# A float32 transformer trunk on one core: the high parts of the mixers' and cross attention's weights written by GpSimd in place of ScalarE

## The chip, the cores and the metric

The kernel runs on one core of a Trainium2 chip. A core has five engines that work at the same time, each through its own queue of instructions in order: TensorE (PE, with PEld for its weight loads), VectorE (DVE), ScalarE (ACT), GpSimd (POOL) and SyncE (SP), which here issues the DMAs. The metric is the device time of one execution in microseconds, as the median of several runs.

## The reference

The kernel computes two layers of a transformer trunk in float32 over 512 tokens of width 1024. A layer is a mixer, a cross attention over 256 memory tokens, and a SwiGLU block of width 2816, each with a norm ahead of it and one behind it:

```python
for layer in range(DEPTH):                       # DEPTH = 2
    h = rms_norm(x, g[0])
    y = even_mixer(h, ...) if layer % 2 == 0 else diff_mixer(h, ...)
    x = x + rms_norm(y, g[1])
    mem_n = rms_norm(mem, mem_norm_g[layer])
    y = memory_cross_attention(rms_norm(x, g[2]), mem_n, wq, wk, wv, wo)
    x = x + rms_norm(y, g[3])
    y = (silu(rms_norm(x, g[4]) @ wg) * (rms_norm(x, g[4]) @ wu)) @ wd
    x = x + rms_norm(y, g[5])
```

The even mixer joins eight heads of attention with a forget gate to eight heads that attend to compressed, selected and windowed keys; the odd mixer has eight heads of differential attention (the difference of two softmaxes).

## The kernel before

Every matrix product is made of three fast float32r products. A value is split in two: the high part hi is the value rounded to float32r, the low part lo is the value less hi, and `mm` (L495) adds hi by hi, hi by lo and lo by hi. So each weight is split once, after it is loaded. `wunit` (L505) issues the DMA of 1024 columns of weights into one of three tiles `raw` and calls `split` (L542), which until now has ACT write hi (a Copy, or a Copy with a factor per partition where the weights take a norm's gain with them, tile `gc`) and DVE write lo (`tensor_sub`, or one instruction that multiplies and subtracts). hi and lo lie in eight tiles `w`, so four pairs; one pair of the output projection lies in the spare end of `hThi` and `hTlo`. `split` also splits what comes out of PSUM: scores, projections and transposed blocks. PSUM sources come from `turn`, `put_PT`, `proj_v` and others, not through `wunit`.

The work comes in this order: the even mixer with its cross attention (to some 380 us in the profile), the first SwiGLU (to 720), the odd mixer with its cross attention (to 1040), the second SwiGLU (to the end). In a mixer the projections and heads come first; at its end, four blocks of 128 tokens go through output projection, norm, cross attention and the next norm one behind the other (`chain`, L871), and the weights of the output projection (eight pairs of tiles), of the keys and values of the memory and of the query (with `gc`) and of the cross attention's output (two pairs) are split near there. In SwiGLU the first two of 22 chunks go through `wunit`, the others through a scheme of seven products with splits of its own (`fast`, L1059).

The order of the instructions is not that of the code. Class `Plan` records every operation with what it depends on, prices each one (`price`, L180), and a list scheduler of 60 passes (`forward`, `backward`, `order`) sets the order in which each engine gets them; all are then issued from one line, so every row of the profile has L477 and rows are told apart by their tiles. For GpSimd `price` has 222 ns and 0.84 ns an element, and 100 ns more with two operands read per partition; nothing in it stands for two engines in each other's way. POOL works at the norms (a power of -0.5, `c<-c,mhalf`), at the softmaxes (the factor on a row, `q<-q,c`), at the last norm of the odd mixer (`x<-q,c`) and sets tiles to zero.

Of the kernel before, what the change touches and what calls it, by code (L numbers as in the profile page):

```python
# [14 lines left out]
AF = mybir.ActivationFunctionType  # L15
# [464 lines left out]
class Trunk:  # L480
    def __init__(self, ctx, tc, a, out):
        self.tc, self.a, self.out = tc, a, out
        self.nc = Plan(tc.nc)
        self.sb = ctx.enter_context(tc.tile_pool(name="sb", bufs=1))
        self.ps = ctx.enter_context(tc.tile_pool(name="ps", bufs=1, space=PSUM))
        self.loads = []


    def bank(self):
# [15 lines left out]
    def wunit(self, pieces, n, where=None, rows=None, raw=None):  # L505

        nc = self.nc
        raw = raw or self.tile([P, 1024], F32, "raw", 3)
        for dst, src in pieces:
            self.loads.append(nc.sync.dma_start(dst(raw), src))  # L510
        if where is None:
            hi, lo = [self.tile([P, 1024], F32R, "w", 8) for k in ("hi", "lo")]
        else:
            hi, lo = where()
        if rows is None:
            self.split(hi[:, :n], lo[:, :n], raw[:, :n])
        else:
            c = n // len(rows)
            for k, f in enumerate(rows):
                s = slice(k * c, (k + 1) * c)  # L520
                self.split(hi[:, s], lo[:, s], raw[:, s], f)
        return hi, lo

    def w_cols(self, w, c0, nko, cols, ko0, rows=None, where=None):
# [14 lines left out]
        units = [self.w_cols(w, c0, min(per, k1 - k), cols, k) for k in range(k0, k1, per)]  # L539
        return lambda ko: tuple(t[:, (ko - k0) % per, :] for t in units[(ko - k0) // per])  # L540

    def split(self, hi, lo, src, scale=None):  # L542
        nc = self.nc
        if scale is None:
            nc.scalar.activation(hi, src, AF.Copy)
            nc.vector.tensor_sub(lo, src, hi.bitcast(F32))
        else:
            nc.scalar.activation(hi, src, AF.Copy, scale=scale)
            nc.vector.scalar_tensor_tensor(lo, src, scale, hi.bitcast(F32), op0=ALU.mult, op1=ALU.subtract)

    def twice(self, hi, lo, src, keys=True):
# [470 lines left out]
    def ffn(self, l, x, ops):  # L1022
        nc, a = self.nc, self.a
        hT, S = ops["hT"], ops["S"]
        blocks = {"A11": [t[:, 0:4, 0:256] for t in hT], "A12": [t[:, 4:8, 0:256] for t in hT],
                  "A22": [t[:, 4:8, 256:512] for t in hT], "S3": [t[:, 0:4, 256:512] for t in hT],
                  "S1": S[1], "S2": S[2], "S4": S[4]}
        groups = [list(range(c, min(c + 3, NCH))) for c in range(0, NCH - 1, 3)]
        groups[-1].append(NCH - 1)
        acts = {}  # L1030

        def up(c):
            wg = self.w_group(a["ffn_wg"][l], c * P, P)
            wu = self.w_group(a["ffn_wu"][l], c * P, P)
            pg, pu = self.bank(), self.bank()
            parts = [slice(0, 256), slice(256, 512)] if c < 2 else [slice(0, 512)]
            for s in parts:
                for ps, wf in ((pg, wg), (pu, wu)):
                    for ko in range(KO):
                        self.mm(ps[:, s], wf(ko), (hT[0][:, ko, s], hT[1][:, ko, s]), ko == 0, ko == KO - 1)  # L1040
            finish(c, pg, pu)

        def finish(c, pg, pu):
            th, b = self.qtile(), self.qtile()
            nc.scalar.activation(th, pg, AF.Tanh, scale=0.5)
            nc.vector.scalar_tensor_tensor(th, th, 1.0, pg, op0=ALU.add, op1=ALU.mult)
            nc.vector.scalar_tensor_tensor(b, th, 0.5, pu, op0=ALU.mult, op1=ALU.mult)
            at = acts[c] = self.unit()
            nc.scalar.activation(at[:, 0:512], b, AF.Copy)
            nc.vector.tensor_sub(at[:, 512:1024], b, at[:, 0:512].bitcast(F32))  # L1050

        def third():

            for i in range(2):
                cs = slice(i * P, (i + 1) * P)
                hi, lo = blocks["S3"]
                self.split(hi[:, :, cs], lo[:, :, cs], ops["keep"][i][:, 0:512].rearrange("p (a b) -> p a b", b=P))

        def fast(c):  # L1059

            rows = lambda w: w[l].rearrange("(ko p) c -> p ko c", p=P)[:, :, c * P:(c + 1) * P]
            raw = []
            for w in ("ffn_wg", "ffn_wu"):
                raw.append(self.tile([P, 1024], F32, "raw", 3))
                self.loads.append(nc.sync.dma_start(raw[-1].rearrange("p (k c) -> p k c", c=P), rows(a[w])))
            (b11, b21), (b12, b22) = [(r[:, 0:512], r[:, 512:1024]) for r in raw]
            t1, t2, t3, t4 = [self.qtile() for _ in range(4)]
            nc.vector.tensor_sub(t1, b12, b11)
            nc.vector.tensor_sub(t2, b22, t1)
            nc.vector.tensor_sub(t3, b22, b12)  # L1070
            nc.vector.tensor_sub(t4, b21, t2)
            G, U, W = self.bank(), self.bank(), self.bank()[:, 0:256]
            G0, G1, U0, U1 = G[:, 0:256], G[:, 256:512], U[:, 0:256], U[:, 256:512]

            def product(ps, left, right, first):
                wt = self.tile([P, 1024], F32R, "w", 8)
                hi, lo = wt[:, 0:512], wt[:, 512:1024]
                self.split(hi, lo, right)
                ah, al = blocks[left]
                for k in range(4):  # L1080
                    s = slice(k * P, (k + 1) * P)
                    self.mm(ps, (hi[:, s], lo[:, s]), (ah[:, k, :], al[:, k, :]), first and k == 0, k == 3,
                            not first and k == 0, skip_group_check=not first)

            product(G0, "A11", b11, True)
            product(U0, "S2", t2, True)
            copies, w7 = self.qtile(), self.qtile()[:, 0:256]
            p1, u2 = copies[:, 0:256], copies[:, 256:512]
            nc.scalar.activation(p1, G0, AF.Copy)
            nc.vector.tensor_add(U0, U0, p1)  # L1090
            nc.scalar.activation(u2, U0, AF.Copy)
            product(W, "S3", t3, True)
            nc.scalar.activation(w7, W, AF.Copy)
            product(G0, "A12", b21, False)
            product(U0, "S1", t1, False)
            nc.vector.tensor_add(U1, U0, w7)
            product(W, "A22", t4, False)
            product(U0, "S4", b22, False)
            nc.vector.tensor_add(G1, W, u2)
            finish(c, G, U)  # L1100

        def make(c):
            if c == PLAIN:
                third()
            (up if c < PLAIN else fast)(c)

        where = self.pt_tiles
        yacc = None
        make(0)
        for gi, grp in enumerate(groups):  # L1110
            last = gi == len(groups) - 1
            for c in grp[1:]:
                make(c)
            wds = []
            for i, c in enumerate(grp):
                wt = where if i < 2 else (lambda: [self.unit(), self.unit()])
                wds.append(self.wunit([(lambda r: r, a["ffn_wd"][l][c * P:(c + 1) * P, :])], 1024, wt))
            if last:
                g = self.gain(a["sandwich_g"][l, 5:6, :])
            else:  # L1120
                make(groups[gi + 1][0])
            if yacc is None:
                yacc = [self.unit(F32) for _ in range(NT)]
            for tb in range(NT):
                s = slice(tb * P, (tb + 1) * P)
                sl = slice(512 + tb * P, 512 + (tb + 1) * P)
                cols = [slice(0, 512), slice(512, 1024)]
                if last and l == 1 and tb == NT - 1:
                    cols = [slice(0, 512), slice(512, 768), slice(768, 1024)]
                for col in cols:  # L1130
                    ps = self.bank()[:, :col.stop - col.start]
                    for j, c in enumerate(grp):
                        self.mm(ps, (acts[c][:, s], acts[c][:, sl]), tuple(t[:, col] for t in wds[j]),
                                j == 0, j == len(grp) - 1)
                    yv = yacc[tb][:, col]
                    if gi == 0:
                        nc.scalar.activation(yv, ps, AF.Copy)
                    else:
                        nc.vector.tensor_add(yv, ps, yv)
                if last:  # L1140
                    self.post_norm([yacc[tb][:, c] for c in cols], g, x, tb)
                    yield tb


# [588 lines left out]
```

## Time and profile before

| | us |
|---|---|
| median of 3 runs | 1384.59 (1384.05 to 1385.82) |
| the profiled execution's own time | 1384.3 |
| its span | 1382.6 |
| PE busy in it | 1349.1 |
| DVE busy | 1114.1 |
| ACT busy | 861.1 |
| POOL busy | 198.9 |

An engine is busy while it has an instruction in work. PE's matmuls are pipelined and their ends are modelled, so that a busy PE isn't always at its best rate. [...]

### The profile page before, as it was taken

To read this page: it belongs to the slowest core of one execution; us is meant where nothing else is said; L and a number is where in the kernel's file an instruction comes from. 1 tells how busy PE (TensorE), PEld (TensorE's weight loads), DVE (VectorE), ACT (ScalarE), POOL (GpSimd) and SP (SyncE) were. 2 spreads that over 40 slices of the span, in tenths; PEclk is the share of its full clock that TensorE was granted. 3 is DMA by queue.
4 is the path that set the end of the run, shared out by engine and by line. 5 is a ranking of instruction groups with operands and counts; after the bars stand their busy time and mean duration, and the time that the engine had idled before them with its cause. 6 is when DMAs were issued, how large, how long until landed. Compare 5 with 4: busy or idle time off the path is not lost.

```text
span 1382.6 us, 25404 instructions
## 1 busy us (share of the span) xinstructions
PE 1349.1 (98%) x9411; PEld 1241.1 (90%) x9411; DVE 1114.1 (81%) x2493; ACT 861.1 (62%) x1954; POOL 198.9 (14%) x307
## 2 busy tenths in 40 slices
PE   7999999999999999999999999999999999999997
PEld 6788987888799999999989999988879999999996
DVE  6767899589898797788786788885999779778976
ACT  5758878588866345335455778795886635533542
POOL 2103224343300000000010232311430000000000
PEclk9999999999999999999999999999999999999999
DMA  7251103312134343334332231343222434332431
GB/s 225 66 154 48 47 17 107 123 47 92 40 89 135 90 123 107 92 92 123 117 113 62 80 105 47 92 151 120 66 62 80 134 92 123 107 92 84 124 99 61
DMA packets 150444, 132.29 MB, mean 96 GB/s; under 512 B 6928, under 2 KB 134096, under 8 KB 150320
## 3 DMA queue, kind: packets, MB, share of 16 engines
q1 hardware_dynamic: 150320, 130.67, 31.3%
q8 instruction: 74, 1.21, 0.4%
q14 instruction: 50, 0.41, 0.1%
HBM read 126.26 MB, written 4.19 MB: 94 GB/s over the span
## 4 chain that ended last, share of the span: by engine, by line
PE 80%; DVE 10%; ACT 4%; DMA 2%; POOL 2%; issue 2%; SPq 0%; POOLq 0%; DVEq 0%; ACTq 0%
PE ps L477 80%; DVE q L477 3%; DVE x L477 2%; DVE u L477 2%; DVE w L477 1%; POOL c L477 1%; ACT q L477 1%; ACT junk L477 1%; DVE pt L477 1%; DVE c L477 1%; DVE hTlo L477 1%; ACT w L477 1%; ACT pt L477 1%; ACT u L477 0%; DMA raw<-in_ffn_wu_dram 0%
## 5 line engine op out<-in xcount | busy, mean ns | idle before, releaser
L477 PE MATMUL ps<-hThi,w 128*128 128x256 f32 (+1 forms) x1664 | 339.4, 292 | 0.6 <-ACT w L477 0.3
L477 PE MATMUL ps<-w,hThi 128*128 128x256 f32 (+2 forms) x1280 | 281.7, 315 | 2.3 <-ACT hThi L477 1.7
L477 PEld LDWEIGHTS ps<-hThi,w 128*128 128x128 f32 x1664 | 272.4, 191 | 7.6 <-ACT w L477 0.5
L477 PE MATMUL ps<-hTlo,w 128*128 128x256 f32 (+1 forms) x832 | 242.2, 292 | 1.0 <-DVE hTlo L477 1.0
L477 PE MATMUL ps<-pt,u 128*128 128x512 f32 (+3 forms) x1126 | 232.5, 338 | 2.0 <-DVE pt L477 1.4
L477 PEld LDWEIGHTS ps<-w,hThi 128*128 128x128 f32 x1280 | 209.7, 191 | 15.1 <-ACT hThi L477 2.4
L477 PEld LDWEIGHTS ps<-pt,u 128*128 128x128 f32 (+1 forms) x1126 | 172.8, 173 | 30.9 <-DVE pt L477 2.6
L477 PE MATMUL ps<-w,hTlo 128*128 128x256 f32 (+2 forms) x640 | 199.1, 312 | 0.0
L477 DVE TENSOR_TENSOR u<-ps,u 128x512 f32<-128x512 f32 (+6 forms) x278 | 149.7, 545 | 57.3 <-PE ps L477 36.7
L477 PE MATMUL ps<-u,w 128*128 128x256 f32 x1440 | 193.3, 283 | 0.9 <-DVE ps L477 0.7
L477 ACT ACTIVATE q<-ps 128x256 f32<-128x256 f32 (+5 forms) x282 | 120.5, 428 | 113.8 <-PE ps L477 94.1
L477 DVE TENSOR_TENSOR w<-raw,w 128x512 fp32r<-128x512 f32 (+2 forms) x193 | 170.1, 885 | 23.3 <-ACT w L477 18.0
L477 PE MATMUL ps<-u 128*128 128x512 f32 (+4 forms) x806 | 185.6, 347 | 1.2 <-DVE x L477 0.7
L477 PEld LDWEIGHTS ps<-u,w 128*128 128x128 f32 x1440 | 181.7, 192 | 3.0 <-DVE ps L477 2.1
L477 ACT ACTIVATE w<-raw 128x512 fp32r<-128x512 f32 (+2 forms) x193 | 149.9, 786 | 55.3 <-DMA raw<-in_ffn_wg_dram 18.8
L477 PEld LDWEIGHTS ps<-hTlo,w 128*128 128x128 f32 x832 | 159.2, 191 | 4.7 <-DVE hTlo L477 1.6
L477 ACT ACTIVATE u<-ps 64x256 fp32r<-64x256 f32 (+5 forms) x277 | 120.2, 443 | 50.2 <-PE ps L477 46.8
L477 PEld LDWEIGHTS ps<-u 128*128 128x128 f32 (+1 forms) x806 | 128.5, 182 | 19.3 <-ACT u L477 1.3
L477 ACT ACTIVATE w<-q 128x512 fp32r<-128x512 f32 x160 | 98.4, 629 | 49.6 <-PE ps L477 22.3
L477 PEld LDWEIGHTS ps<-w,hTlo 128*128 128x128 f32 x640 | 122.1, 191 | 6.6 <-DVE hTlo L477 0.2
L477 POOL TENSOR_TENSOR c<-c,mhalf 128x1 f32<-128x1 f32 (+1 forms) x68 | 54.8, 807 | 502.9 <-DVE c L477 500.7
L477 DVE TENSOR_TENSOR w<-q,w 128x512 fp32r<-128x512 f32 x160 | 107.2, 686 | 22.8 <-ACT w L477 21.0
(151 smaller groups left out, 1909.7 us busy)
## 6 DMA issues: line engine op xcount, KB each, us to landing
raw<-in_ffn_wg_dram SPq DMA_DIRECT2D x44, 512.0 KB
raw<-in_ffn_wu_dram SPq DMA_DIRECT2D x44, 512.0 KB
raw<-in_ffn_wd_dram SPq DMA_DIRECT2D x44, 512.0 KB
raw<-in_od_w_in_dram SPq DMA_DIRECT2D x24, 512.0 KB
raw<-in_ev_w_in_dram SPq DMA_DIRECT2D x16, 512.0 KB
u<-in_sandwich_g_dram SPq DMA_DIRECT2D x10, 512.0 KB
x<-in_x_dram SPq DMA_DIRECT2D x8, 512.0 KB
raw<-in_ev_w_out_dram SPq DMA_DIRECT2D x8, 512.0 KB
```

Of the source, the lines that this page charges most:

```text
L477: getattr(getattr(self.nc, self.eng[i]), method)(*args, **kw)
```

## The change

A flag `mixing` says whether the code that is being recorded belongs to a mixer with its cross attention; it is set false at the start of SwiGLU and true again behind it. `wunit` gives it to `split`, which then has GpSimd write hi: a `tensor_copy` to float32r in place of ACT's Copy, a `tensor_scalar` with the factor in place of ACT's Copy with a factor. DVE's instruction for lo is as it was. Splits from PSUM and all of SwiGLU's stay on ACT.

```diff
--- before.py
+++ after.py
@@ -484,6 +484,7 @@
         self.sb = ctx.enter_context(tc.tile_pool(name="sb", bufs=1))
         self.ps = ctx.enter_context(tc.tile_pool(name="ps", bufs=1, space=PSUM))
         self.loads = []
+        self.mixing = True
 
 
     def bank(self):
@@ -513,12 +514,12 @@
         else:
             hi, lo = where()
         if rows is None:
-            self.split(hi[:, :n], lo[:, :n], raw[:, :n])
+            self.split(hi[:, :n], lo[:, :n], raw[:, :n], pool=self.mixing)
         else:
             c = n // len(rows)
             for k, f in enumerate(rows):
                 s = slice(k * c, (k + 1) * c)
-                self.split(hi[:, s], lo[:, s], raw[:, s], f)
+                self.split(hi[:, s], lo[:, s], raw[:, s], f, pool=self.mixing)
         return hi, lo
 
     def w_cols(self, w, c0, nko, cols, ko0, rows=None, where=None):
@@ -539,13 +540,20 @@
         units = [self.w_cols(w, c0, min(per, k1 - k), cols, k) for k in range(k0, k1, per)]
         return lambda ko: tuple(t[:, (ko - k0) % per, :] for t in units[(ko - k0) // per])
 
-    def split(self, hi, lo, src, scale=None):
+    def split(self, hi, lo, src, scale=None, pool=False):
+
         nc = self.nc
         if scale is None:
-            nc.scalar.activation(hi, src, AF.Copy)
+            if pool:
+                nc.gpsimd.tensor_copy(hi, src)
+            else:
+                nc.scalar.activation(hi, src, AF.Copy)
             nc.vector.tensor_sub(lo, src, hi.bitcast(F32))
         else:
-            nc.scalar.activation(hi, src, AF.Copy, scale=scale)
+            if pool:
+                nc.gpsimd.tensor_scalar(hi, src, scale, 1.0, op0=ALU.mult, op1=ALU.mult)
+            else:
+                nc.scalar.activation(hi, src, AF.Copy, scale=scale)
             nc.vector.scalar_tensor_tensor(lo, src, scale, hi.bitcast(F32), op0=ALU.mult, op1=ALU.subtract)
 
     def twice(self, hi, lo, src, keys=True):
@@ -1025,6 +1033,7 @@
         blocks = {"A11": [t[:, 0:4, 0:256] for t in hT], "A12": [t[:, 4:8, 0:256] for t in hT],
                   "A22": [t[:, 4:8, 256:512] for t in hT], "S3": [t[:, 0:4, 256:512] for t in hT],
                   "S1": S[1], "S2": S[2], "S4": S[4]}
+        self.mixing = False
         groups = [list(range(c, min(c + 3, NCH))) for c in range(0, NCH - 1, 3)]
         groups[-1].append(NCH - 1)
         acts = {}
@@ -1139,6 +1148,7 @@
                         nc.vector.tensor_add(yv, ps, yv)
                 if last:
                     self.post_norm([yacc[tb][:, c] for c in cols], g, x, tb)
+                    self.mixing = True
                     yield tb
 
 
```

The instructions that change engine make the scheduler set a new order on all engines. Three places follow. In the rows, x4 is four alike in a row; a CAST is the copy to float32r.

POOL at the end of the even mixer, where the last blocks go through their norms. Before:

```order
L477 TENSOR_TENSOR c_914<-c_914,mhalf 128x1
L477 TENSOR_TENSOR c_928<-c_928,mhalf 128x1
L477 TENSOR_TENSOR c_933<-c_933,mhalf 128x1
L477 TENSOR_TENSOR c_951<-c_951,mhalf 128x1
L477 TENSOR_TENSOR c_946<-c_946,mhalf 128x1
L477 TENSOR_TENSOR c_960<-c_960,mhalf 128x1
L477 TENSOR_SCALAR q<-q,c_972 128x256 x2
```

Now:

```order
L477 TENSOR_TENSOR c_914<-c_914,mhalf 128x1
L477 TENSOR_TENSOR c_928<-c_928,mhalf 128x1
L477 TENSOR_TENSOR c_933<-c_933,mhalf 128x1
L477 CAST w<-raw 128x1024
L477 TENSOR_TENSOR c_946<-c_946,mhalf 128x1
L477 TENSOR_TENSOR c_951<-c_951,mhalf 128x1
L477 TENSOR_TENSOR c_960<-c_960,mhalf 128x1
L477 TENSOR_SCALAR q<-q,c_972 128x256 x2
```

A copy of 1024 columns (the second half of the cross attention's output weights) now stands between two norms' powers.

POOL where the odd mixer's last heads begin; `c_2205` and `c_2214` are norms of the memory, `nlam` is the factor of the second softmax. Before:

```order
L477 TENSOR_TENSOR c_2172<-c_2171,mhalf 128x2
L477 TENSOR_SCALAR x<-q,c_2172 128x128 x2
L477 TENSOR_TENSOR c_2205<-c_2205,mhalf 128x1
L477 TENSOR_TENSOR c_2214<-c_2214,mhalf 128x1
L477 TENSOR_SCALAR q<-q,c_2220,nlam 128x128
L477 TENSOR_SCALAR q<-q,c_2235,nlam 128x256
L477 TENSOR_SCALAR q<-q,c_2249,nlam 128x256
L477 TENSOR_TENSOR c_2239<-c_2238,mhalf 128x2
L477 TENSOR_SCALAR x<-q,c_2239 128x128 x2
L477 TENSOR_SCALAR q<-q,c_2276,nlam 128x384
```

Now:

```order
L477 TENSOR_TENSOR c_2205<-c_2205,mhalf 128x1
L477 TENSOR_TENSOR c_2172<-c_2171,mhalf 128x2
L477 TENSOR_SCALAR q<-q,c_2220,nlam 128x128
L477 TENSOR_SCALAR q<-q,c_2235,nlam 128x256
L477 TENSOR_SCALAR x<-q,c_2172 128x128
L477 TENSOR_TENSOR c_2214<-c_2214,mhalf 128x1
L477 TENSOR_SCALAR x<-q,c_2172 128x128
L477 CAST w<-raw 128x1024 x3
L477 CAST hThi<-raw 128x1024
L477 CAST w<-raw 128x1024 x2
L477 TENSOR_SCALAR q<-q,c_2249,nlam 128x256
L477 TENSOR_TENSOR c_2239<-c_2238,mhalf 128x2
```

Six copies in a row now stand ahead of the softmax factor of `c_2249` and the power of `c_2239`.

ACT at the same place; `hThi` with `subg` is the heads' output on its way to the output projection. Before:

```order
L477 ACTIVATE q<-ps,c_2205 128x256
L477 ACTIVATE hThi<-ps,subg 128x512
L477 ACTIVATE u<-ps,c_2205 128x256
L477 ACTIVATE pt<-ps 128x128
L477 ACTIVATE hThi<-ps,subg 128x512
L477 ACTIVATE w<-raw 128x1024 x2
L477 ACTIVATE q<-ps,c_2214 128x256
L477 ACTIVATE u<-ps 64x2x128 x4
L477 ACTIVATE u<-ps,c_2214 128x256
L477 ACTIVATE pt<-ps 128x128
L477 ACTIVATE pt<-ps 128x256
L477 ACTIVATE w<-raw 128x1024
```

Now:

```order
L477 ACTIVATE hThi<-ps,subg 128x512 x2
L477 ACTIVATE q<-ps,c_2205 128x256
L477 ACTIVATE u<-ps,c_2205 128x256
L477 ACTIVATE pt<-ps 128x128
L477 ACTIVATE q,c_2246<-q,c_2246 128x256
L477 ACTIVATE q<-ps,c_2214 128x256
L477 ACTIVATE u<-ps 64x2x128 x4
L477 ACTIVATE u<-ps,c_2214 128x256
L477 ACTIVATE pt<-ps 128x128
L477 ACTIVATE hThi<-ps,subg 128x512 x2
L477 ACTIVATE pt<-ps 128x256
```

The three copies of weights are gone from between the splits of the heads' output and of the softmax blocks.

## Rows read from the trace of the kernel before

**Rows 1.** The page: span, and busy time of each engine.

```profile
span 1382.6 us, 25404 instructions
...
PE 1349.1 (98%) x9411; PEld 1241.1 (90%) x9411; DVE 1114.1 (81%) x2493; ACT 861.1 (62%) x1954; POOL 198.9 (14%) x307
```

**Rows 2.** Busy time by stretch: length, then PE, PEld, DVE, ACT, POOL; clock; DMA share, GB/s.

```profile
0.00:20.00 20.00, 10.55 (x54) 9.38 (x55) 11.02 (x25) 13.14 (x28) 8.32 (x28) 1.00 0.95 297
160.00:220.00 60.00, 55.93 (x431) 50.61 (x430) 56.82 (x238) 46.26 (x135) 17.70 (x30) 1.00 0.14 45
300.00:380.00 80.00, 74.81 (x567) 66.69 (x566) 71.16 (x140) 65.60 (x170) 27.15 (x36) 1.00 0.18 56
380.00:720.00 340.00, 339.39 (x2356) 317.19 (x2355) 282.40 (x461) 171.18 (x312) 5.74 (x7) 1.00 0.37 110
720.00:900.00 180.00, 179.58 (x1474) 177.16 (x1473) 141.14 (x455) 126.60 (x351) 43.88 (x67) 1.00 0.24 74
900.00:940.00 40.00, 38.65 (x220) 33.08 (x220) 30.69 (x84) 35.01 (x92) 7.10 (x13) 1.00 0.40 132
960.00:1040.00 80.00, 76.09 (x568) 67.54 (x568) 75.05 (x151) 67.80 (x184) 28.22 (x40) 1.00 0.27 80
1040.00:1358.00 318.00, 317.65 (x2239) 298.94 (x2238) 260.12 (x423) 157.25 (x282) 0.00 (x0) 1.00 0.34 102
```

**Rows 3.** The page: the chain that ended last, share of the span by engine.

```profile
PE 80%; DVE 10%; ACT 4%; DMA 2%; POOL 2%; issue 2%; SPq 0%; POOLq 0%; DVEq 0%; ACTq 0%
```

**Rows 4.** Groups by form: ACT's splits that write hi of weights: busy, mean ns.

```profile
L477 ACT ACTIVATE w<-raw 128x1024 fp32r<-128x1024 f32 x70 | 72.4, 1054 | 12.4 <-DMA raw<-in_od_w_in_dram 6.5 <-DMA raw<-in_ev_cmp_w_v_dram 1.8 <-DMA raw<-in_od_w_out_dram 1.5
L477 ACT ACTIVATE w<-raw,gc 128x512 fp32r<-128x512 f32 x16 | 11.0, 715 | 0.0
L477 ACT ACTIVATE w<-raw,gc 128x256 fp32r<-128x256 f32 x16 | 6.8, 498 | 1.1 <-PE ps L477 1.1
```

**Rows 5.** Timeline of POOL, factors on 512 and 128 columns: start, length, [idle before <-releaser].

```profile
111.13 0.69 POOL L477 TENSOR_SCALAR q<-q,c 128x512 f32<-128x512 f32 x1 [0.71 <-DVE c L477]
...
121.86 0.37 POOL L477 TENSOR_SCALAR q<-q,c 128x128 f32<-128x128 f32 x1 [10.03 <-DVE c L477]
```

**Rows 6.** Timeline of PE at the start: what a matmul waited for.

```profile
17.69 0.50 PE L477 MATMUL ps<-w,hThi 128*128 128x512 f32 x1 [0.54 <-ACT w L477]
```

**Rows 7.** Timeline of ACT in the odd mixer's last heads.

```profile
900.27 1.33 ACT L477 ACTIVATE w<-raw,gc 128x512 fp32r<-128x512 f32 x2
...
914.16 0.68 ACT L477 ACTIVATE hThi<-ps,subg 128x512 fp32r<-128x512 f32 x1
...
917.72 0.71 ACT L477 ACTIVATE hThi<-ps,subg 128x512 fp32r<-128x512 f32 x1
918.29 2.03 ACT L477 ACTIVATE w<-raw 128x1024 fp32r<-128x1024 f32 x2
...
930.39 1.06 ACT L477 ACTIVATE w<-raw 128x1024 fp32r<-128x1024 f32 x1
```

**Rows 8.** Timeline of POOL, a factor on 512 columns beside a DVE split.

```profile
168.63 1.61 POOL L477 TENSOR_SCALAR q<-q,c 128x512 f32<-128x512 f32 x1 [1.19 <-issue]
```

**Rows 9.** Timeline of DVE at the same time.

```profile
168.39 1.21 DVE L477 TENSOR_TENSOR w<-raw,w 128x1024 fp32r<-128x1024 f32 x1
```

**Rows 10.** Timeline of POOL, three factors in a row at 305 us.

```profile
304.72 2.88 POOL L477 TENSOR_SCALAR q<-q,c,gates 128x512 f32<-128x512 f32 x3 [4.39 <-DVE c L477]
```

**Rows 11.** Timeline of DVE there: one instruction twice.

```profile
305.94 1.01 DVE L477 TENSOR_TENSOR x<-x,u 128x512 f32<-128x512 f32 x1
...
308.53 0.68 DVE L477 TENSOR_TENSOR x<-x,u 128x512 f32<-128x512 f32 x1
```

**Rows 12.** Groups by form: DVE's low parts of 1024 columns of weights.

```profile
L477 DVE TENSOR_TENSOR w<-raw,w 128x1024 fp32r<-128x1024 f32 x70 | 85.1, 1224 | 14.4 <-ACT w L477 9.8 <-PE ps L477 2.0 <-issue 1.6
```

**Rows 13.** The chain of waits at the even mixer's end: pieces that are POOL's.

```profile
314.26 1.54 POOL c L477
...
326.82 1.06 POOL c L477
...
370.07 1.54 POOL c L477
```

## The prediction

> **What bounds the kernel now.** I read the busy time of the engines first, then the same by stretch, then the chain of waits, and last the timelines of the stretches that are not full. On the page PE is busy for 1349.1 of 1382.6 us and ACT for 861.1 [rows 1], so the engine that is relieved isn't the one that is full. The table by stretch says where that leaves room: PE idles 20.00 - 10.55 = 9.45 us in the first 20 us, 4.07 from 160 to 220, 5.19 from 300 to 380, 1.35 from 900 to 940 and 3.91 from 960 to 1040, but only 0.6 and 0.35 in the two long stretches of SwiGLU, and 0.4 in the 180 us of the odd mixer's heads [rows 2]. So nothing that is done in SwiGLU or in those heads can show, and all that the mixers have to give behind the start is 4.07 + 5.19 + 1.35 + 3.91 = 14.5 us.
>
> Which engine is full there is read in the same rows. From 160 to 220 DVE works 56.82 of 60 us, from 300 to 380 71.16 of 80, from 960 to 1040 75.05 of 80; ACT has 46.26, 65.60 and 67.80. Only from 900 to 940 is it the other way, ACT 35.01 and DVE 30.69 of 40 [rows 2]. The chain that ended last agrees: behind PE's 80% come DVE with 10%, ACT with 4%, POOL with 2% [rows 3]. DVE's work isn't changed. The change takes load from the second engine, and the question is how much of 14.5 us was the second engine's.
>
> **What moves.** 71 copies of up to 1024 columns leave ACT (of the 70 in the group, the eight of SwiGLU's first chunks stay; four from `pt`, two into `hThi` and three short ones at the start join), and 32 products with a factor. At 1.054, 0.715 and 0.498 us [rows 4] that is at most 71 x 1.054 + 16 x 0.715 + 16 x 0.498 = 94 us of ACT in the mixers.
>
> POOL's price for them isn't in the trace: it has written no float32r so far. Its factor on 512 columns takes 0.69 us and on 128 columns 0.37 [rows 5], so 0.32 / 384 = 0.83 ns a column and, drawn on, 0.69 + 512 x 0.00083 = 1.12 us for 1024. I take 1.12, 0.69 for the 512 of a factor and 0.48 for 256; together at most 71 x 1.12 + 16 x 0.69 + 16 x 0.48 = 98 us. As an upper end I keep 1.61 us, which a POOL instruction of half the size takes when it is hindered [rows 8]; as the lower, ACT's 1.05. [...]
>
> **The terms, against the profiled execution's 1384.3 us.**
>
> The start: the first matmul of 512 columns waits 0.54 us for ACT's copy [rows 6], which stood behind four squares for the norms in ACT's queue. On POOL it doesn't. I take -0.5; the rest of the first 20 us is loads, which no copy hastens. Ends: 0 and -0.5, since that wait is all there is.
>
> From 900 to 940: between 900.27 and 931 ACT has four products (4 x 0.715) and six copies (6 x 1.054), 9.2 us [rows 4, 7]. Two copies at 918.29 take 2.03 us right behind the fourth of the splits of the heads' output (`hThi` with the gain, the first of them at 914.16) and ahead of the last two [rows 7]; in the new order no copy of weights stands between these splits. ACT is the full engine here, and its load falls to 26 of 40 us or less, so I take all of PE's idle time, -1.3. Ends: 0 and -1.35.
>
> From 160 to 220: six products of 0.715 us leave, 4.3 us of ACT's 46.26 [rows 2, 4]. DVE stays at 56.82, so the bound hardly moves; but DVE waits for ACT's results in between. I take a third of 4.07, -1.4. Ends: 0, and -4.07.
>
> From 300 to 380 and 960 to 1040: two copies leave ACT in each (the cross attention's output weights); the four of SwiGLU's first chunks stay on ACT. 2 x 2 x 1.054 = 4.2 us of ACT leave, of the 133 there. PE idles 9.1 us in both [rows 2]. I take -1.5 together; ends 0 and -4.2.
>
> The price on DVE: POOL and DVE get in each other's way where DVE reads two inputs from SBUF. A factor on 512 columns took 1.61 us and not 0.69 when DVE had begun the low part of 1024 columns 0.24 us before it [rows 5, 8, 9]; and the other way, DVE's `x<-x,u` took 1.01 us at 305.94, while POOL had three factors in work, and 0.68 at 308.53 [rows 10, 11]. So far DVE lost little: its 70 low parts of 1024 columns average 1.224 us against the 1.21 of one [rows 9, 12]. In the three stretches that DVE fills, ten copies and products now read beside it, 6 x 0.69 + 4 x 1.12 = 8.6 us. If DVE stood for all of it, +8.6; by its average so far, nearly 0. Rows 12 have the more cases, and I take +0.6.
>
> [...]
>
> The price on POOL's own queue: each copy waits for its load, and what is queued behind it waits too. That is the power of a norm behind a copy at the end of each mixer, and six copies ahead of a softmax factor in the odd mixer. These powers stand in the chain there, at 1.06 to 1.54 us a piece [rows 13]. Next after them come DVE's norm products and PE's transposes. In both mixers a copy of 1.12 us could be added once, and stretched to 1.61: from 0 to +3.2. Since the order has each copy's weights loaded early, I take +0.6. Behind a low part that comes late, SP's queue holds the next load, since a `raw` tile is free only when both halves are read; ACT's copies waited 6.5 us on loads of the odd mixer's weights [rows 4], in heads where PE idles 0.4 us, so this is covered; without the cover it would be those 6.5 us once.
>
> Sum: -0.5 - 1.3 - 1.4 - 1.5 + 0.6 + 0.6 = -3.5, so 1380.8. The median of the runs is 0.3 above the profiled execution, which gives 1381.1. About 0.2%, 2.8 us, is what a measurement of this kernel can tell from no change; the forecast lies just beyond.
>
> **Rivals.**
>
> DVE pays for it: in the three stretches that it fills, its instructions with two inputs from SBUF stand behind POOL's copies. For it: rows 8 to 11 show the wait, DVE has 3.2, 8.8 and 5.0 us to spare in them, and POOL's instructions there get longer than any that DVE met so far. Against it: in rows 8 and 9 it was POOL that stood, and the order's copies can fall into DVE's waits. With two thirds of 8.6 us, 5.7, with 1.2 on POOL's queue and only the first two gains (-1.8), the sum is +5.1: 1389.7 on the runs' median. It decides from the point where both prices together pass the gains of 4.7 by 2.8, at 7.5 us, or sooner if the gains are less. A quarter.
>
> Nothing to be told: ACT wasn't the bound where DVE is full, the gains there vanish, -1.8 + 1.2 = -0.6, so 1384.0. For it: rows 2 as they stand. Against it: DVE and ACT take turns in one chain, and 4% of the chain is ACT's [rows 3].
>
> A larger gain: the new order draws work out of the full stretches. With both ends of the gains, -0.5 - 1.35 - 4.07 - 4.2 = -10.1, 1374.5. Against it: DVE is as full as before.
>
> The copy doesn't do what it is there for: at 1.61 us, six in a row take 9.7 us where ACT took 6.3, the weights come 3.4 us late once, and the gain of 3.5 is gone: 1384.5. This counts with "nothing to be told".
>
> **How the numbers follow.** The forecast has 0.35, the larger gain 0.08, nothing to be told 0.29 (the slow copy in it with 0.05), DVE's price 0.24, and 0.04 are for a copy that waits for its load ahead of the norms in both mixers and adds more than 3.2 us. So faster 0.43, same 0.29, slower 0.28. The range goes from 1373 (just beyond the larger gain) to 1390 (just beyond DVE's price) and leaves out about one in seven; the forecast's own is 1376 to 1381.8.
>
> **What would show it.** Right, if in the profile after ACT's total falls by 85 to 94 us and POOL's rises by 95 to 130, copies of 1024 columns average 1.1 to 1.4 us, PE's idle time from 900 to 940 is gone, and DVE's low parts stay at 1.22 us. DVE's price would show as low parts and norm sums that average over 1.3 us, and as idle time of PE in the three stretches that grows. If SwiGLU's stretches change by more than 1 us each, the order there moved, which this sum doesn't hold.

## The result: 10 us slower, and the profile after

The changed kernel takes 1394.72 us, median of 4 runs (1394.28 to 1395.36), the kernel before 1384.32 beside it; the ratio is 1.0073, 95% interval 1.006 to 1.0085. The forecast was 1381.1, so both the sign and the range are wrong.

The page of the changed kernel first: span, busy time by engine, and the chain by engine.

```profile
span 1392.6 us, 25420 instructions
...
PE 1350.7 (97%) x9411; PEld 1241.6 (89%) x9411; DVE 1134.0 (81%) x2493; ACT 780.3 (56%) x1851; POOL 310.5 (22%) x410
...
PE 73%; DVE 14%; ACT 4%; issue 4%; DMA 3%; POOL 2%; SPq 0%; POOLq 0%; DVEq 0%; ACTq 0%
```

Against [rows 1] the load moved much as the sum said: ACT has 80.8 us less, POOL 111.6 more. But DVE, none of whose instructions was changed, works 19.9 us longer, and in the chain DVE has 14% where it had 10 [rows 3].

The table by stretch (length, then PE, PEld, DVE, ACT, POOL, clock, DMA share, GB/s), of the stretches of [rows 2] and two more, 20 to 60 and 220 to 300 us:

```profile
0.00:20.00 20.00, 10.17 (x51) 8.65 (x51) 11.17 (x26) 10.09 (x25) 11.16 (x31) 1.00 0.89 269
20.00:60.00 40.00, 37.12 (x197) 30.07 (x197) 26.55 (x95) 13.16 (x33) 14.22 (x15) 1.00 0.29 78
160.00:220.00 60.00, 56.56 (x458) 52.69 (x457) 55.85 (x244) 43.41 (x131) 22.16 (x36) 1.00 0.09 28
220.00:300.00 80.00, 77.98 (x478) 67.48 (x477) 60.13 (x174) 46.56 (x126) 45.93 (x53) 1.00 0.31 106
300.00:380.00 80.00, 75.26 (x585) 68.33 (x583) 76.10 (x160) 68.26 (x185) 30.27 (x42) 1.00 0.20 60
380.00:720.00 340.00, 338.97 (x2359) 317.35 (x2359) 282.63 (x457) 168.18 (x306) 9.57 (x11) 1.00 0.37 111
720.00:900.00 180.00, 179.58 (x1465) 176.67 (x1464) 147.17 (x447) 102.68 (x317) 70.48 (x91) 1.00 0.23 71
900.00:940.00 40.00, 38.02 (x235) 32.69 (x233) 34.07 (x91) 28.42 (x86) 16.36 (x24) 1.00 0.40 133
960.00:1040.00 80.00, 74.53 (x528) 64.86 (x527) 71.80 (x146) 62.53 (x173) 34.63 (x49) 1.00 0.23 73
1040.00:1358.00 318.00, 316.98 (x2250) 298.90 (x2249) 262.45 (x427) 160.06 (x287) 1.77 (x2) 1.00 0.34 103
```

Two stretches of the kernel before that the rows ahead of the prediction don't have:

```profile
20.00:60.00 40.00, 40.00 (x215) 33.49 (x214) 29.48 (x108) 24.23 (x49) 6.43 (x10) 1.00 0.31 89
...
220.00:300.00 80.00, 79.83 (x510) 69.47 (x509) 59.10 (x185) 61.30 (x155) 30.73 (x40) 1.00 0.30 100
```

PE was full in both and now idles 2.88 and 2.02 us. Matched instruction by instruction, PE runs 4.9 us late when the odd mixer's heads begin (730.5, not 725.6), 5.3 near their end (882.6, not 877.3), and 9.1 in the middle of the second SwiGLU (1192.6, not 1183.5). Already at 60 us of the span it is 5.0 us late. So about half is lost before the first SwiGLU, next to nothing in it or in the heads, and the rest behind 900. ACT's load from 900 to 940 fell from 35.01 to 28.42 us, and PE's idle time there didn't go, it grew from 1.35 to 1.98.

Two things are seen in the trace. The first is in the groups by form (busy us, mean ns of one, idle before them and what ended it):

```profile
L477 DVE TENSOR_TENSOR w<-raw,w 128x1024 fp32r<-128x1024 f32 x70 | 93.7, 1346 | 19.3 <-POOL w L477 8.5 <-issue 4.9 <-ACT w L477 2.2
L477 POOL CAST w<-raw 128x1024 fp32r<-128x1024 f32 x62 | 77.3, 1255 | 430.8 <-DVE u L477 316.2 <-PE ps L477 92.5 <-DMA raw<-in_od_w_in_dram 7.2
L477 POOL TENSOR_SCALAR w<-raw,gc 128x256 fp32r<-128x256 f32 x16 | 9.3, 598 | 9.9 <-PE ps L477 9.9
L477 DVE SCALAR_TENSOR_TENSOR w<-raw,gc,w 128x256 fp32r<-128x256 f32 x16 | 10.1, 688 | 11.1 <-POOL w L477 11.1
L477 DVE TENSOR_TENSOR pt<-ps,pt 128x512 fp32r<-128x512 f32 x64 | 42.9, 684 | 3.1 <-ACT pt L477 2.6
```

DVE's low parts of 1024 columns average 1346 ns and not 1224 [rows 12]; those of 256 columns 688 (480 before). POOL's copy averages 1255 ns, though 43 of all its 68 copies of 1024 columns take under 1.1 us. The last line is the control: `pt<-ps,pt` reads one of its inputs from PSUM and takes the 684 ns that it took before:

```profile
L477 DVE TENSOR_TENSOR pt<-ps,pt 128x512 fp32r<-128x512 f32 x64 | 43.1, 684 | 5.2 <-ACT pt L477 4.9
```

After the change 30 of these 64 run beside an instruction of POOL's that reads SBUF, and they average 685 ns; the other 34 average 683. The timeline of the first weights shows how low parts and copies meet; POOL's rows, then DVE's:

```profile
32.45 1.91 POOL L477 CAST w<-pt 128x1024 fp32r<-128x1024 f32 x1 [9.98 <-issue]
...
34.35 1.99 POOL L477 CAST w<-pt 128x1024 fp32r<-128x1024 f32 x1
...
43.19 4.00 POOL L477 CAST w<-raw 128x1024 fp32r<-128x1024 f32 x2 [6.80 <-PE ps L477]
```

```profile
32.23 3.20 DVE L477 TENSOR_TENSOR w<-pt,w 128x1024 fp32r<-128x1024 f32 x2 [0.56 <-PE ps L477]
...
43.08 3.20 DVE L477 TENSOR_TENSOR w<-pt,w 128x1024 fp32r<-128x1024 f32 x2 [7.64 <-PE ps L477]
```

DVE's low part that began first (32.23) took 1.2 us and POOL's copy beside it 1.91 and not 1.04; then the copy in work made the next low part take 1.95. The two of them go as if in turn.

The second is at 23 us, and there no copy of POOL's is near. DVE, PE and ACT of the changed kernel:

```profile
23.03 0.16 DVE L477 CAST q<-pos_i 128x4 f32<-128x4 int32 x1
25.85 0.29 DVE L477 TENSOR_TENSOR q<-q 128x128 f32<-128x128 f32 x1 [2.65 <-DMA q<-in_od_lambda_dram]
```

```profile
27.70 0.24 PE L477 MATMUL ps<-ident,q 32*128 32x32 f32 x1
30.25 0.76 PE L477 MATMUL ps<-w,hThi 128*128 128x288 f32 x3 [2.31 <-ACT hThi L477]
```

```profile
29.00 0.35 ACT L477 ACTIVATE q<-q 128x32 f32<-128x32 f32 x2 [0.59 <-DVE q L477]
...
29.59 1.08 ACT L477 ACTIVATE hThi<-ps 128x512 fp32r<-128x512 f32 x2
```

In the new order DVE's product on `od_lambda`, which the odd mixer needs 700 us later, stands ahead of the rope tables. Its load is issued 3.35 us later than before (19.78, not 16.43), since those of the row gains now go ahead of it, so DVE waits 2.65 us; the sines on ACT come late behind the tables (29.00), behind them in ACT's queue the split of `hThi` (29.59), and PE waits 2.31 us. In the kernel before the tables start at 22.76 and the product at 25.43, and PE waits for nothing there:

```profile
22.76 1.37 DVE L477 TENSOR_SCALAR q<-q 128x8 f32<-128x8 f32 x10
...
25.43 0.29 DVE L477 TENSOR_TENSOR q<-q 128x128 f32<-128x128 f32 x1 [0.29 <-PE ps L477]
```

### The profile page after: what moved, and what is told of

Same layout as the page of the kernel before. It is cut to its first block, busy times and chain, and to the rows that moved or that the text cites. A ratio compares the mean times of both kernels' runs of the same rounds, so it can differ in the third digit from the quotient of the medians.

```text
span 1392.6 us, 25420 instructions
## 1 busy us (share of the span) xinstructions
PE 1350.7 (97%) x9411; PEld 1241.6 (89%) x9411; DVE 1134.0 (81%) x2493; ACT 780.3 (56%) x1851; POOL 310.5 (22%) x410
## 4 chain that ended last, share of the span: by engine, by line
PE 73%; DVE 14%; ACT 4%; issue 4%; DMA 3%; POOL 2%; SPq 0%; POOLq 0%; DVEq 0%; ACTq 0%
PE ps L477 73%; DVE w L477 3%; DVE q L477 3%; DVE u L477 2%; DVE x L477 2%; DVE pt L477 2%; DVE c L477 1%; ACT q L477 1%; POOL c L477 1%; DMA raw<-in_ev_w_in_dram 1%; ACT junk L477 1%; DMA raw<-in_ffn_wd_dram 1%; ACT u L477 1%; POOL q L477 1%; ACT pt L477 1%
## 5 line engine op out<-in xcount | busy, mean ns | idle before, releaser
L477 DVE TENSOR_TENSOR w<-raw,w 128x512 fp32r<-128x512 f32 (+2 forms) x193 | 178.7, 930 | 24.5 <-POOL w L477 10.2
L477 POOL CAST w<-raw 128x1024 fp32r<-128x1024 f32 (+2 forms) x65 | 80.3, 1243 | 434.4 <-DVE u L477 316.2
L477 ACT ACTIVATE u<-ps 64x256 fp32r<-64x256 f32 (+6 forms) x277 | 119.9, 442 | 73.6 <-PE ps L477 69.8
L477 PEld LDWEIGHTS ps<-u 128*128 128x128 f32 (+1 forms) x806 | 129.3, 182 | 19.9 <-DVE u L477 1.3
```

Source lines behind the costliest of these rows:

```text
L477: getattr(getattr(self.nc, self.eng[i]), method)(*args, **kw)
```

## The experiments

Theory A: POOL reading SBUF beside DVE is the loss, whatever the order. Theory B: the new order is. Theory C: copies come late by their place in POOL's queue, or by their wait for a load. The order of a kernel is the planner's; in several runs it is planned for one engine and issued on another, so that PE's and DVE's instructions keep one order word for word.

**The order of before, POOL writes.**

```
 if pool:
-    nc.gpsimd.tensor_copy(hi, src)
+    op = nc.scalar.activation(hi, src, AF.Copy)          # planned as ACT's
+    op["real"] = "gpsimd", "tensor_copy", (hi, src), {}  # issued on POOL; products alike
```

> The order is planned as if the copies and products were still ACT's, so that TensorE and VectorE run exactly the order of before; only the engine that writes the high parts is GpSimd. Theory A (VectorE and GpSimd slow each other where both read SBUF, whatever the order): it stays slower than before by 7 to 12 us, 1391 to 1396, and the low parts that lie beside a copy take 1.4 us or more instead of 1.2. Theory B (the loss is the new order: VectorE's product on od_lambda, which waits for its DMA at 27 us, and the odd mixer's end): at most 3 us over before, 1383 to 1387. Theory C (the copies come late since they stand behind other work in GpSimd's queue): with an order that does not know of that queue it gets worse than the changed kernel, 1396 to 1405, and TensorE's idle time ends with GpSimd.

1399.98 us, ratio 1.011 (1.0096 to 1.0124): worse than with its own order, above what A allowed and inside the range of C. B falls as the whole cause. The table by stretch, DVE, POOL and PE about 242 us:

```profile
220.00:300.00 80.00, 77.04 (x456) 65.59 (x455) 58.54 (x166) 43.17 (x119) 40.01 (x50) 0.98 0.30 98
```

```profile
241.96 4.89 DVE L478 TENSOR_TENSOR w<-raw,w 128x1024 fp32r<-128x1024 f32 x2
```

```profile
241.16 1.52 POOL L478 TENSOR_SCALAR q<-q,c,gates 128x512 f32<-128x512 f32 x2
242.62 1.04 POOL L478 CAST w<-raw 128x1024 fp32r<-128x1024 f32 x1
243.60 1.04 POOL L478 CAST hThi<-raw 128x1024 fp32r<-128x1024 f32 x1
```

```profile
244.59 0.36 PE L478 MATMUL ps<-pt,u 128*128 128x256 f32 x1
247.12 0.33 PE L478 MATMUL ps<-u 128*128 128x128 f32 x1 [2.17 <-DVE c L478]
```

Of the two low parts in the DVE row, the first runs from 241.96 to 245.72: 3.75 us. It begins while a factor is in work, two copies follow on POOL without a gap (each 1.04 us, none slowed), and the low part ends 1.08 us after the last of them. So it stood through three instructions of POOL's, not one, and PE, which had 79.83 of this stretch's 80 us full before, waits 2.17 us for the sums of masked scores (`c`) behind it. The granted clock of this stretch, as a share of full speed, is 0.98, where it was 1.00. That is some 1.6 us more, an estimate: 0.02 of its 80 us.

**The new order, ACT writes.** The edit turned round: planned as POOL's, issued on ACT.

```
+    op = nc.gpsimd.tensor_copy(hi, src)
+    op["real"] = "scalar", "activation", (hi, src, AF.Copy), {}
```

> The order is planned as for GpSimd, so that TensorE and VectorE run exactly the order of the changed kernel, but the copies and products are issued on ACT. A: within 3 us of before, 1382 to 1387, since nothing new runs beside VectorE. B: 1391 to 1396, as the changed kernel, since the order is its own. From the traces so far some 2.3 us at 27 to 31 us are order (VectorE waits there for a DMA) and should stay in either case: so A with that stall is 1386 to 1388. C: as A.

1402.66 us, ratio 1.0134 (1.012 to 1.0148): a miss for A and above what B allowed. PE waits 3.8 us for ACT until 30.94 us, and idles 5.42 us from 900 to 940. Its low parts average 1231 ns, so next to nothing of A can be in its 18 us. I read it so: an order made for a light ACT puts copies where a loaded ACT is late. No run tests this, and the run does not tell A from B.

**One mixer alone**, planned anew for it: POOL only before the first SwiGLU (the line that sets `mixing` true again is left out), and only after it (`mixing` starts false).

> GpSimd writes the high parts before the first SwiGLU alone (even mixer, cross attention of its layer); from there on ACT does, and the order is planned for that. In the changed kernel about 5 of the 10 us had come by 60 us of the span and 5 more between 905 and 1060. If each loss belongs to its own part of the program, this gives 1388 to 1391. If the loss is a matter of the order as a whole (B), it can come out anywhere between 1380 and 1395.

> ACT writes the high parts before the first SwiGLU, GpSimd after it (odd mixer, its layer's cross attention). If each loss belongs to its own part, 1388 to 1391, and together with the run on the even mixer alone the two losses add up to about 10 us. If the stretch of 905 to 1060 lost only because the start had shifted what ran there, 1383 to 1386.

1396.69 us, ratio 1.009 (1.0076 to 1.0104), and 1392.64, ratio 1.0059 (1.0046 to 1.0073). Both lie above the 1388 to 1391 of losses that belong to their own parts, and 12 and 8 us don't add up to 10: each plan is another order, and halves of different orders can't be summed. From here on orders were kept.

**The same orders, with POOL only filling.**

```
+    op["real"] = "gpsimd", "memset", (hi.bitcast(F32), 0.0), {}
```

> The changed kernel in its own order, but where GpSimd copied or multiplied it now fills the high part with zeros: the same tiles, widths and places in its queue, without reading SBUF and without waiting for the weight's DMA. (The high parts are left out of the result.) What is left over before is then the order alone. Theory A (both engines reading SBUF slow each other): the low parts come back to 1.22 us, and of the 10 us over before some 5 go, 1388 to 1391; the stall at 27 to 31 us behind od_lambda stays. Theory B (all of it is the order): 1393 to 1396.

> The order of before, as in the run that kept it, with GpSimd filling the high parts with zeros instead of copying or multiplying (the high parts are left out of the result). That run was 15.5 us over before. A: nearly all of that goes, 1383 to 1388, since order and queue are the same and only the reading beside VectorE is gone; the one low part that took 3.75 us at 242 us of the span comes back to 1.22. Theory C (the copies come late by their place in GpSimd's queue, or by the way of a signal from GpSimd): it stays over 1393.

In the order of before: 1385.6 us, ratio 1.0001 (0.9992 to 1.0009). The whole loss of 15 us is gone with the reading. Its groups by form:

```profile
L478 DVE TENSOR_TENSOR w<-raw,w 128x1024 fp32r<-128x1024 f32 x70 | 85.4, 1228 | 14.3 <-POOL w L478 4.6 <-issue 2.9 <-DMA raw<-in_ev_w_in_dram 2.7
L478 POOL MEMSET w<- 128x1024 f32 x66 | 61.9, 954 | 405.6 <-DVE w L478 307.2 <-PE ps L478 98.4
```

POOL is nearly as busy with 1024 columns (954 ns each, in the same places of its queue) and DVE's low parts are back at 1228. In the new order: 1388.59, ratio 1.0025 (1.0017 to 1.0034); what is left there is the wait at the start, in this run 3.6 us, and a fall of the granted clock around it: its mean is 0.95 from 20 to 30 us and 0.71 in the 10 us from 30 us on:

```profile
30.00:40.00 10.00, 9.59 (x40) 8.39 (x41) 4.22 (x7) 0.84 (x2) 2.13 (x4) 0.71 0.00 1
```

**POOL reads, but doesn't wait.** A fill neither reads nor waits for a load, so the last two could still be C.

```
+    i = self.ident[:, None, 0:c].to_broadcast([P, n // c, c])
+    op["real"] = "gpsimd", "tensor_copy", (hi, i), {}
```

> As the run in the order of before with zeros filled in, but GpSimd now reads while it writes: each copy or product becomes a copy of the same width from the 128x128 identity, which lies in SBUF from the start, so that it does not wait for the weight's DMA. (The high parts are left out of the result.) Beside the run with zeros only the reading is new, beside the run with the real copies only the wait for the DMA is gone. A (reading beside VectorE): 1396 to 1402, low parts that lie beside a copy over 1.4 us on average again. If it was GpSimd's wait for the weight's DMA that held up its queue: 1384 to 1388.

1398.69 us, ratio 1.0104 (1.009 to 1.0118). The wait for the load is gone and the loss is there:

```profile
L478 DVE TENSOR_TENSOR w<-raw,w 128x1024 fp32r<-128x1024 f32 x70 | 99.5, 1432 | 11.1 <-PE ps L478 4.8 <-POOL w L478 2.1 <-issue 1.9
L478 POOL CAST w<-ident 128x1024 fp32r<-128x1024 f32 x66 | 84.3, 1293 | 397.5 <-DVE w L478 306.4 <-PE ps L478 90.7
```

C falls, A stands: at equal order, place and width, reading alone makes about 14 us (1.0104 against 1.0001). Waiting for the loads adds nothing that shows (1.0104 against 1.011 with the real copies). It is DVE's slowed work that costs here, and not a DVE that waits longer for POOL's high parts: before its low parts DVE idles 2.1 us for them in this run and 4.6 with the fills. Of PE's own waits, those that end with DVE add up to 26.4 us here and to 18.4 with the fills, those that end with POOL to 2.8 and 2.1.

**The product on `od_lambda` later**, in the finished order of the changed kernel.

```
-    for i in self.order():
+    for i in self.later(self.order()):   # product, sum, exp, nlam: behind the row gains
```

> The changed kernel with one edit to the finished order: VectorE's product on od_lambda and the four instructions behind it (nlam) run after the row gains instead of ahead of the rope tables, so that VectorE doesn't wait 2.65 us at 23 to 26 us for that load. If the new order's loss at the start is this wait, TensorE's wait of 2.3 us at 28 to 30 us goes and the time is 1391.9 to 1393; if the wait only moves on (the next load or table is late in its place), it stays within 0.7 us of 1394.7.

1392.42 us, ratio 1.0043 (1.003 to 1.0057). PE no longer waits for ACT at 30 us. By the medians it is worth the 2.3 us expected; by the ratios (1.0073 less 1.0043) about 4 us, and each of the two intervals reaches some 1.8 us to either side.

**Both: new order, fill, product later.**

> Both in one: the changed kernel's order with zeros filled in (3.5 us over before) and the product on od_lambda moved behind the row gains (it gave 2.3 us by itself). The high parts are left out of the result. If the two causes add up: 1386 to 1387, so that of the 10 us some 6 are reading beside VectorE, 2.3 the wait for od_lambda, and 1 to 2 the rest of the order. If the fill had hidden the wait already: 1388 to 1389.

1382.63 us, ratio 0.9987 (0.9978 to 0.9995): faster than before by about 2 us, and lower than a sum of the two causes would have it. The difference from the run with fill alone, 6 us, is that run's wait of 3.6 and its clock; here the clock is 1.00 at the same place:

```profile
30.00:40.00 10.00, 9.73 (x48) 8.05 (x47) 2.23 (x2) 0.00 (x0) 1.64 (x4) 1.00 0.00 1
```

This run and the one with the product later alone have one order on every engine, and differ only in what POOL does, real copies (L483) or fills (L484). DVE's low parts in both, then two stretches, with copies and with fills:

```profile
L483 DVE TENSOR_TENSOR w<-raw,w 128x1024 fp32r<-128x1024 f32 x70 | 93.3, 1340 | 20.9 <-POOL w L483 10.2 <-issue 4.8 <-ACT w L483 2.2
L484 DVE TENSOR_TENSOR w<-raw,w 128x1024 fp32r<-128x1024 f32 x70 | 85.8, 1231 | 17.5 <-issue 4.7 <-POOL w L484 3.4 <-ACT w L484 2.2
```

```profile
220.00:300.00 80.00, 77.95 (x485) 67.65 (x484) 60.08 (x178) 47.50 (x129) 46.88 (x54) 1.00 0.30 102
300.00:380.00 80.00, 75.18 (x570) 68.06 (x570) 74.64 (x154) 66.79 (x180) 29.65 (x41) 0.98 0.20 60
```

```profile
220.00:300.00 80.00, 79.48 (x510) 69.78 (x509) 59.23 (x182) 50.54 (x138) 41.96 (x56) 1.00 0.29 92
300.00:380.00 80.00, 75.21 (x575) 68.72 (x574) 73.97 (x145) 64.34 (x172) 27.12 (x37) 0.98 0.22 65
```

With copies PE idles 1.53 us more from 220 to 300 us, 1.10 more from 60 to 160 and 1.25 more from 900 to 940, but only 0.13, 0.03 and 0.58 more in the three stretches that DVE fills. (The clock of 0.98 from 300 to 380 is in both.) DVE also idles longer for POOL's high parts before its low parts, 10.2 us and not 3.4.

**Where it costs, in the order of before:** the odd mixer's `od_w_in` alone (24 copies), and the whole even mixer alone.

```
+    self.mine = w.tensor.name == "in_od_w_in_dram"       # od_w_in alone
-    self.mixing = True                                   # even mixer alone: not set again
```

> The order of before; GpSimd copies the high parts of od_w_in alone (24 of the 68 copies of 1024 columns), ACT the others. These fall mostly between 720 and 905 us, where TensorE is busy for 179.58 of 180 us and VectorE has room. If slowed low parts cost only where TensorE would wait for what stands behind them: 1383.5 to 1386.5, although the low parts there are as slow as in the changed kernel (1.4 us beside a copy). If every slowed low part costs its excess: VectorE's excess of these 24 copies is some 4 us, 1388 to 1389.

> The order of before; GpSimd takes over before the first SwiGLU alone. In the run that kept the order for the whole program TensorE was 9.6 us late at the first SwiGLU's start and 13.4 at the end. If the even mixer's part is where reading beside VectorE costs: 1393 to 1397, with a low part of 3 us or more at about 242 us. If that came from how things happened to stand in that run: 1385 to 1390.

1385.73 us, ratio 1.0007 (0.9998 to 1.0016), and 1395.11, ratio 1.0076 (1.0063 to 1.0088). In the first, POOL's 24 copies average 1325 ns and DVE works 5.6 us longer from 720 to 900 than in [rows 2], and nobody waits for it:

```profile
720.00:900.00 180.00, 179.58 (x1471) 177.04 (x1471) 146.73 (x450) 103.30 (x318) 70.57 (x89) 1.00 0.24 74
```

In the second the low part at 243.4 us again takes 3.78 us, and PE waits 2.19.

**A search of the order by itself:** the kernel before, with the planner's price of a POOL instruction 30 ns higher.

> The kernel before, with the planner's price of a GpSimd instruction raised by 30 ns and nothing else: a new search of the order with the copies still on ACT. It tells how far a search alone moves the time. If the order of before is an ordinary one, 1383 to 1387. If it is a lucky one among many, and a good part of the 10 us is the loss of it, 1388 to 1396.

1385.21 us, ratio 1.0 (0.9991 to 1.0008). The order of before isn't one that every new search loses.

The account then, by medians: 1384.6 for the kernel before; -2.0 for the new order and the lighter ACT (the last fill); +9.8 for the reading (1382.63 to 1392.42, one order, copies for fills); +2.3 for the product on `od_lambda`. That is 1394.7, as measured. By the ratios to the kernel before, the same three are -1.8, +7.8 and +4.2. So the reading costs some 8 to 10 us and the product 2 to 4. Two things go with the reading when POOL fills: its wait for the load, and its own copies' being late where DVE holds them up. In the old order neither shows; in the new order they weren't told apart from DVE's slowed work. No version with real copies was run as an improvement: even without any price the gain is 2 us.

## Why the prediction was wrong

**The step that failed is the price on DVE, +0.6.** With what POOL's waits and late copies add in the new order, reading beside DVE measured 8 to 10 us there, and 14 to 15 in the old. Its direction and mechanism were right, in rows 8 to 11; the size failed in two places. First, "by its average so far" took DVE's 1.224 us [rows 12] as evidence that DVE rarely pays. But by the trace only 14 of the 70 ran beside an instruction of POOL's that reads, none of them beside a copy of weights, and they average 1.235 us. After, 45 of the 70 do and average 1.42: the 16 that meet only POOL's other work average 1.23, as before, and the 29 that meet a copy or a product of weights 1.52, up to 2.06. A copy on POOL can read the next `raw` tile just while the low part of the tile before is made. So the factors on rows were no measure of what copies would do. Second, the upper end of 8.6 counted only copies in the three stretches that DVE fills. With one order, copies against fills, these three hold 0.7 us of PE's added idle time, and the stretches of 60 to 160, 220 to 300 and 900 to 940 us hold 3.9. PE waits for the one instruction behind a slowed one, not for DVE's sum. The plainest case is in the old order, not in the changed kernel: the low part of 3.75 us at 242 us, in a stretch where DVE works 59 of 80 us. It stood through three POOL instructions and took 2.5 us more than the 1.22 of one alone, where the upper end counts 1.12 us for a copy.

The prediction gave the mechanism of rows 8 to 11 as the main price a quarter. The runs show with which instructions it costs time here. In the order of before, DVE's low parts, with two inputs in SBUF, average 1432 ns with POOL's copies from the identity and 1228 with fills, which read nothing. DVE's sum with one input in PSUM averages 685 ns beside POOL's reads in the changed kernel, and 683 without them. That one DVE instruction stands through three of POOL's in a row is shown by the run in the old order, with its 3.75 us.

**The rival on DVE's price** had the mechanism and 1389.7; it too looked in the three stretches. In these PE's idle time sums to 13.2 us before (4.07, 5.19, 3.91) and 13.7 after (3.44, 4.74, 5.47); most of the loss lies outside them. (These stretches are fixed in time, and after the change the work in them is 5 to 9 us late.)

**The gains, -4.7,** are about 2, in the new order with fills. In the order of before, relief of ACT without a price is worth nothing (1.0001). From 900 to 940, where ACT was the full engine, PE's idle time is 0.96 us in that run and 1.25 in the last fill, not 0: though ACT is no longer full there, the waits of PE's that are left end with ACT (0.4 and 1.3 us) and with DVE (0.5 and 0.2) in the heads' chain. The start gives its -0.5 in the fills (8.94 us idle in the old order, 9.45 before), but in the changed kernel PE idles 9.83 us there.

**The price on POOL's queue, +0.6,** wasn't seen as a term of its own in the old order: the fill keeps the queue's order and loses nothing, and the wait for the loads adds nothing to the reading. In the new order it stays open.

**The order** had no term. The 2 to 4 us on `od_lambda` are such a thing: DVE's new order has the product ahead of the tables, and the prediction had looked at ACT's and POOL's queues alone.

**Right, or nearly so, were** ACT's relief (80.8 us, a little below the 85 to 94 named), POOL's load (111.6 us of 95 to 130), the copy's price (1.04 us unhindered, 1.12 taken), and SwiGLU's stretches, where PE's busy time moved by less than 1 us.

## What to carry to other kernels

Work that moves to GpSimd is priced with what VectorE does beside it: count VectorE's instructions that read two inputs from SBUF (here the low parts: 1432 ns with copies that read, 1228 with fills) in every stretch, not only where VectorE is full, and ask who waits for each; reads back to back on GpSimd can stand in their way as one piece, as the low part of 3.75 us shows. Put such copies where TensorE has its inputs long ahead, as `od_w_in` here (1385.73 us, ratio 1.0007), or leave them on ACT. When a planner reorders, read every engine's new order up to the first load that it waits for; one instruction for much later can hold a short queue, as the product on `od_lambda` did (2.65 us of VectorE's wait, 2.31 of TensorE's).

## What the hardware showed that I had not expected

A GpSimd copy of 1024 columns from float32 to float32r takes 1.04 us where nothing hinders it, no more than ACT's 1.054 and a little less than the 1.12 drawn on from the factors' 0.83 ns a column [rows 5]. A fill of 1024 columns takes 0.954 us and costs VectorE beside it nothing that shows (low parts of 1228 ns, and 1224 before). TensorE's granted clock had a mean of 0.71 from 30 to 40 us in the run whose wait of 3.6 us ended at 30.4 us, and of 0.83 in the run with the new order on ACT, whose wait of 3.8 us ended at 30.94; behind the wait of 2.31 us of the changed kernel it was 1.00.
